# Hybrid trunk in fp32: squares of the keys from the diagonal of the Gram matrix, attention sinks as a 129th score column, another bank for one unit

## The chip, the cores and the metric

The kernel runs on one core of one Trainium2 chip. The metric is the device time of one execution, in microseconds (us). The core's engines are named as in the profile: PE is TensorE (PEld its weight loads), DVE is VectorE, ACT is ScalarE, POOL is GpSimd, and SP is the engine whose queue (SPq) issues nearly all DMAs. The chip may grant TensorE a lower clock; in the profiled run the mean granted clock is 0.999 of full speed.

## What is computed

Two layers of a block with two branches in parallel, then a feed-forward part, for 512 tokens of width 1024, all in float32. Cut to what matters here:

```python
h = rmsnorm(x, pre_mix_g);  proj = h @ w_in          # q k v z, beta, decay | swa q k v | gates A, B
# branch A, gated DeltaNet, 8 heads of 128, per chunk of the sequence:
k = k * rsqrt(sum(k*k) + EPS)                         # l2norm, q likewise
beta = sigmoid(b);  g = cumsum(-exp(a_log) * softplus(a + dt_bias))
L = where(strict, (k*beta) @ k.T * exp(g_i - g_j), 0)
u = triangular_solve(I + L, v * beta);  w = triangular_solve(I + L, k * beta * exp(g))
# branch B, sliding window of 128, 16 query heads on 2 key heads:
m = maximum(max(scores), sink);  p = exp(scores - m)
probs = p / (sum(p) + exp(sink - m));  o = probs @ v
mix = (sigmoid(gate_a) * (o_a @ w_up_dn) + sigmoid(gate_b) * (o_b @ w_up_sw)) @ w_o
x = x + rmsnorm(mix, post_mix_g)
x = x + rmsnorm(relu(rmsnorm(x, pre_mlp_g) @ w_ff1)**2 @ w_ff2, post_mlp_g)
```

## The kernel before

All large products are made in three passes of a shortened fp32 (`mm_a`, L339 to L341): activations and weights are split in a high and a low part, and wh·high, wh·low and wl·high are summed in PSUM, each matmul 128x128 by 512 columns. A unit of 128 output columns has 8 chunks, so 24 such matmuls. The weights come by DMA in tiles of 128x1024 (`wr`); ScalarE makes `wh` from one (L323) and VectorE `wl` (L324), four tiles ahead of use.

A layer runs in stages; times are layer 0's, layer 1's lie 907 us later. Up to 75 us: norm, the projection of branch B's inputs, the decays (`decays`). From 75 to 250 us: the 16 groups of the sliding-window attention (four blocks of 128 tokens, two key heads, two halves of four query heads, numbered 1 to 16 here), mixed by the list MIX with units of the combined projection: K, a head's keys (`k_unit`), G, a unit of gate B (`gb_unit`), A, one of gate A. From 250 to 300 us: the up-projection of branch B (`ps_us`) and two units of gate A. From 300 to 476 us: the eight DeltaNet heads. Then the up-projection of branch A, the output projection and, from 600 us, the feed-forward part.

A group (`att_group`) makes scores for four heads in two banks of the pool PZ, masks them into an SBUF tile M of 128 x 512, takes the row maximum (L904), brings in the sink (`nsk`, its negative; L905, L907, L908, L912), exponentiates with row sums (L910), turns the sums into factors (L913), scales M (L916), has TensorE turn M's four blocks (`ps_pt`, L922), splits the result in `pf_h` and `pf_l`, and multiplies with the values (`ps_o`, L938). The second half of a group, from the transposes on, is written behind the units of the next entry of MIX.

A head's keys: `k_unit` projects (`ps_kp`), convolves, and makes the Gram matrix of the four 128-token blocks (`ps_a`, in the single bank of pool PK). Its diagonal, the keys' squared norms, is taken by four products with the identity with row sums (L740); from it come `irk`, the inverse norm (a pow on GpSimd, L744), and `cj` = beta / (norm² + EPS) (L747, L748). Then `uu` is the Gram matrix times `cj` of the row times the decays D (L752), and is stored (`ud`). When all eight heads are stored, `solve` loads the 32x32 diagonal blocks (`ub`, one DMA of 512 KB in runs of 32 floats) and inverts them column by column on VectorE (pairs L798, L801), between other work, up to the end of the `ps_us` units; the inverses go out to `pd` and come back as `Tc`. For the heads, `d_load` loads `uu` again (`ur`), `d_inverse` completes the inverse by block products on TensorE (`ps_i`), and `d_chain` uses `irk`, `cj` and the decays.

PSUM tiles come from four pools: PM (2 banks, the units), PS (3, general), PK (1), PZ (2). A scheduler orders each engine's instructions by costs of its own out of the program order; where an `Order` object brackets instructions (the four transposes of a group, for one), they stay together. Each engine runs its queue in order, and an instruction that waits holds all behind it; the DMAs of the SP queue are issued in order as well.

Of the kernel before, what the change touches and what calls it, by code (L numbers as in the profile page):

```python
# [15 lines left out]
ALU = mybir.AluOpType  # L16
# [103 lines left out]
def hybrid_trunk(ctx, tc, x, positions, pre_mix_g, dn_conv_w, dn_a_log, dn_dt_bias, dn_norm_g,  # L120
# [139 lines left out]
    gd = dr.tile([32, P], F32, name="gd")  # L260
    sd = dr.tile([H, 512], F32, name="sd")
# [258 lines left out]
    for l in range(depth):  # L520
# [131 lines left out]
        beta = s1("beta", 32)  # L652
# [20 lines left out]
        gc, ngc, neg, egl = (s1(n_, 32) for n_ in ("gc", "ngc", "neg", "egl"))  # L673

        def decays():
# [12 lines left out]
            act(out=egT, in_=gT, func=AF.Exp)  # L688
# [33 lines left out]
        cj, irk = [], []  # L722

        def k_unit(h):
# [55 lines left out]
        def solve():  # L780
# [3 lines left out]
                bass.AP(u0.tensor, u0.offset, [[32 * P + 32, P], [P, 32], [1, 32]]))  # L784
            pb = X4("pb")
# [3 lines left out]
            uv = ub.rearrange("p (j i) -> p j i", j=32)  # L789
            pv = pb.rearrange("p (n i) -> p n i", n=32)  # L790
            for j in range(30, -1, -1):
# [11 lines left out]
                yield  # L803
            dma(pd, pb)
# [65 lines left out]
        def att_group(t, g, e):  # L870
# [12 lines left out]
            M = T[2]("M")  # L883
            for jj in range(2):
# [9 lines left out]
                Mv = c4(M)[:, jj * 2:jj * 2 + 2, :]  # L894
# [9 lines left out]
            nc.vector.tensor_reduce(out=nm, in_=c4(M), axis=AX.X, op=ALU.max, negate=True)  # L904
            tt(out=nm, in0=nm, in1=nsk[:, g, e, :], op=ALU.min)  # L905
            es = sm.tile([P, 4], F32, name="es", bufs=4)
            tt(out=es, in0=nm, in1=nsk[:, g, e, :], op=ALU.subtract)  # L907
            act(out=es, in_=es, func=AF.Exp)  # L908
            for j in range(4):
                act(out=M[:, j * P:(j + 1) * P], in_=M[:, j * P:(j + 1) * P], func=AF.Exp,  # L910
                    bias=nm[:, j:j + 1], accum_out=den[:, j:j + 1])
            tt(out=den, in0=den, in1=es, op=ALU.add)  # L912
            nc.vector.reciprocal(den, den)  # L913
            for j in range(4):
                js = slice(j * P, (j + 1) * P)
                act(out=M[:, js], in_=M[:, js], func=AF.Copy, scale=den[:, j:j + 1])  # L916
# [4 lines left out]
            for j in (3, 0, 1, 2):  # L921
                tr(ps[:, j * P:(j + 1) * P], M[:, j * P:(j + 1) * P], ident)  # L922
# [543 lines left out]
```

## Time and profile before

| | us |
|---|---|
| median of 3 runs | 1830.95 |
| lowest and highest of them | 1829.16, 1831.1 |
| the profiled execution, its own time | 1830.59 |
| its span, first to last instruction | 1828.6 |
| PE busy | 1809.1 (99%) |
| PEld busy | 1503.9 (82%) |
| DVE busy | 1292.1 (71%) |
| ACT busy | 940.9 (51%) |
| POOL busy | 211.2 (12%) |

A matmul is pipelined: the profile draws each longer than the distance to the next, so that PE can be drawn busy where it is not at its peak. The page says that shares are means over stages; the rows further down are of single stages. A wait is put down to the releaser whose event came last. Where a timeline row ends in square brackets, they hold the engine's idle time just ahead of the row and what ended it.

### The profile page before, as it was taken

Reading aid. Unit: us, or ns where it says so; the run is one execution under the profiler, and the core shown is the slowest. Engines: PE = TensorE matmul, PEld = TensorE weight load, DVE = VectorE, ACT = ScalarE, POOL = GpSimd, SP = SyncE. Lnnn points to the kernel's source line nnn. Section 1 sums busy time; section 2 is a strip of 40 time slices with the busy share of each in tenths; the row PEclk is TensorE's granted clock in tenths of the full one; section 3 lists DMA queues with packets and bytes.
Section 4 is the critical chain, followed back from the end, with each engine's and each line's share of the span. In section 5 each row is a group of like instructions: output and inputs, shape, how many; then the busy total and the mean of one; then the engine's idle time right before and its main releaser. Section 6 shows DMA issues by size and latency. Waiting matters only on the chain.

```text
span 1828.6 us, 26748 instructions
## 1 busy us (share of the span) xinstructions
PE 1809.1 (99%) x9598; PEld 1503.9 (82%) x9598; DVE 1292.1 (71%) x2466; ACT 940.9 (51%) x1913; POOL 211.2 (12%) x386
## 2 busy tenths in 40 slices
PE   9999999999999999999999999999999999999998
PEld 8888778888788888888898887888887898888886
DVE  5499796887566758684556997968885568585934
ACT  6678742444434645544347877234444346554442
POOL 0322102221101000000003221022111010000000
PEclk9999999999999999999999999999999999999999
DMA  5633447554453363564245343485545534544631
GB/s 188 202 118 116 115 149 223 179 170 149 124 191 124 96 216 120 168 217 151 93 151 181 104 127 110 167 234 165 160 139 153 172 119 135 174 163 148 233 102 46
DMA packets 146422, 278.48 MB, mean 152 GB/s; under 512 B 33569, under 2 KB 66657, under 8 KB 146290
## 3 DMA queue, kind: packets, MB, share of 16 engines
q1 hardware_dynamic: 145778, 276.75, 47.4%
q8 instruction: 75, 1.23, 0.3%
q14 instruction: 57, 0.47, 0.1%
q0 software_dynamic: 512, 0.03, 0.0%
HBM read 239.38 MB, written 37.36 MB: 151 GB/s over the span
## 4 chain that ended last, share of the span: by engine, by line
PE 84%; DVE 6%; ACT 5%; DMA 3%; issue 1%; POOL 1%; SPq 0%; POOLq 0%; DVEq 0%; ACTq 0%
PE ps_f L340 6%; PE ps_f L339 6%; PE ps_f L341 6%; PE ps_p L402 3%; PE ps_p L404 3%; PE ps_p L400 3%; PE ps_b L388 3%; PE ps_b L387 3%; PE ps_b L389 3%; PE ps_vp L339 2%; PE ps_us L339 2%; PE ps_ud L339 2%; PE ps_vp L341 2%; PE ps_ud L341 2%; PE ps_ud L340 2%; PE ps_us L340 2%
## 5 line engine op out<-in xcount | busy, mean ns | idle before, releaser
L323 ACT CAST wh<-wr 128x1024 fp32r<-128x1024 f32 (+1 forms) x332 | 343.1, 1040 | 542.2 <-PE ps_f L340 145.8
L324 DVE TENSOR_TENSOR wl<-wr,wh 128x1024 fp32r<-128x1024 f32 (+1 forms) x332 | 400.4, 1216 | 303.6 <-ACT wh L323 300.6
L339 PE MATMUL ps_f<-g_h,wh 128*128 128x512 f32 x448 | 174.3, 389 | 0.0
L340 PE MATMUL ps_f<-g_l,wh 128*128 128x512 f32 x448 | 174.3, 389 | 0.0
L341 PE MATMUL ps_f<-g_h,wl 128*128 128x512 f32 x448 | 174.3, 389 | 0.0
L402 PE MATMUL ps_p<-wl,P_h 128*128 128x512 f32 x336 | 131.4, 391 | 0.4 <-DVE wl L324 0.3
L404 PE MATMUL ps_p<-wh,P_l 128*128 128x512 f32 x336 | 130.8, 389 | 0.0
L400 PE MATMUL ps_p<-wh,P_h 128*128 128x512 f32 x336 | 129.5, 389 | 0.0
L437 POOL TENSOR_TENSOR pr<-pq,pw 128x1 f32<-128x1 f32 x16 | 9.8, 613 | 807.6 <-DVE pq L436 807.6
L339 PEld LDWEIGHTS ps_f<-g_h,wh 128*128 128x128 f32 x448 | 84.1, 188 | 17.4
L341 PEld LDWEIGHTS ps_f<-g_h,wl 128*128 128x128 f32 x448 | 84.1, 188 | 17.4
L340 PEld LDWEIGHTS ps_f<-g_l,wh 128*128 128x128 f32 x448 | 84.1, 188 | 17.4
L402 PEld LDWEIGHTS ps_p<-wl,P_h 128*128 128x128 f32 x336 | 63.1, 188 | 15.8 <-DVE wl L324 2.4
L400 PEld LDWEIGHTS ps_p<-wh,P_h 128*128 128x128 f32 x336 | 63.1, 188 | 13.3
L404 PEld LDWEIGHTS ps_p<-wh,P_l 128*128 128x128 f32 x336 | 63.1, 188 | 12.8
L387 PE MATMUL ps_b<-wh,h_h 128*128 128x432 f32 (+1 forms) x192 | 71.1, 370 | 0.0
L388 PE MATMUL ps_b<-wl,h_h 128*128 128x432 f32 (+1 forms) x192 | 70.5, 367 | 0.3 <-DVE wl L324 0.3
L389 PE MATMUL ps_b<-wh,h_l 128*128 128x432 f32 (+1 forms) x192 | 70.2, 366 | 0.0
L293 DVE TENSOR_TENSOR wr<-wr 128x1024 f32<-128x1024 f32 x48 | 58.0, 1220 | 2.6 <-DMA wr<-in_weights_dram 1.9
L340 PE MATMUL ps_qp<-h_l,wh 128*128 128x512 f32 x128 | 54.0, 422 | 0.0
L339 PE MATMUL ps_vp<-h_h,wh 128*128 128x512 f32 x128 | 53.9, 421 | 0.0
L341 PE MATMUL ps_vp<-h_h,wl 128*128 128x512 f32 x128 | 53.6, 419 | 0.0
(359 smaller groups left out, 4873.6 us busy)
## 6 DMA issues: line engine op xcount, KB each, us to landing
wr<-in_weights_dram SPq DMA_DIRECT2D x320, 512.0 KB, 3.5
wr<-in_weights_dram SPq DMA_DIRECT2D x24, 432.0 KB, 3.6
D<-dd SPq DMA_DIRECT2D x32, 256.0 KB, 3.2
xd<-xo SPq DMA_DIRECT2D x12, 512.0 KB, 2.8
xt<-xd SPq DMA_DIRECT2D x24, 256.0 KB, 3.7
D<-gd SPq DMA_DIRECT2D x16, 256.0 KB, 6.5
dd<-D SPq DMA_DIRECT2D x16, 256.0 KB, 3.9
kkd<-kk SPq DMA_DIRECT2D x16, 256.0 KB, 2.0
```

What stands on the lines that cost most here:

```text
L293: tt(out=held[j], in0=held[j], in1=part(i, k, j), op=ALU.add)
L323: nc.scalar.copy(wh[:, :w], wr[:, :w])
L324: sub(out=wl[:, :w], in0=wr[:, :w], in1=wh[:, :w].bitcast(F32), op=ALU.subtract)
L339: mm(ps, lhsT=wh[:, k, :], rhs=hi, start=k == 0, stop=False)
L340: mm(ps, lhsT=wh[:, k, :], rhs=lo, start=False, stop=False)
L341: mm(ps, lhsT=wl[:, k, :], rhs=hi, start=False, stop=k == KT - 1)
L387: mm(pss[t], lhsT=hi[:, tsl], rhs=wh[:, r, :], start=k == 0, stop=False)
L388: mm(pss[t], lhsT=hi[:, tsl], rhs=wl[:, r, :], start=False, stop=False)
L389: mm(pss[t], lhsT=lo[:, tsl], rhs=wh[:, r, :], start=False, stop=k == KT - 1)
L400: mm(pss[t], lhsT=hi[:, c], rhs=wh[:, r, :], start=first, stop=False, skip_group_check=onto)
L402: mm(pss[t], lhsT=hi[:, c], rhs=wl[:, r, :], start=False, stop=False, skip_group_check=onto)
L404: mm(pss[t], lhsT=lo[:, c], rhs=wh[:, r, :], start=False, stop=last, skip_group_check=onto)
```

## The change

The keys' norms are no longer taken per head. `k_unit` makes `uu` = Gram matrix times D in one VectorE product, without `cj`. Since D is 1 on its diagonal, the squared norms stand on the diagonal of `uu`, and `solve` reads them from the blocks `ub` that it loads: it adds EPS (L778 of the new file), stores that through a new DRAM tile `nd`, makes the reciprocal in place (L780), multiplies by beta (`bq`, loaded in the same layout from a new DRAM tile `bd`), scales `ub` by it (L782), and loads `nd` turned as 32x128 (`gT`, a tile used before for the decays). At the end of the column steps TensorE turns that (`ps_nt`), and `irk` and `cj` for all heads are made at once, with one pow on GpSimd of 128x32. `d_load` now has ScalarE scale each block of `ur` by `cj`, four instructions a head. The decays and beta are turned in one transpose of 64 columns (`gcb`), and beta's part is stored to `bd`.

In `att_group` M becomes 128 x 4 x 129. GpSimd copies the sinks into column 128 of the four parts; the maximum and the sums run over 129 columns, and L905, L907, L908 and L912 are gone, as is `nsk`. The scaling and the transposes take the first 128 columns.

The first unit of `ps_us` takes its bank from PS in place of PM.

```diff
         snk = s1("snk", QH)
         dma(snk, sw_sinks[l].partition_broadcast(P))
-        nsk = sm.tile([P, 2, 2, 4], F32, name="nsk", bufs=1)
-        for g in range(2):
-            ts(out=nsk[:, g], in0=snk[:, g * 8:(g + 1) * 8].rearrange("p (j e) -> p e j", e=2),
-               scalar1=-1.0, scalar2=None, op0=ALU.mult)
...
-            tr(ps[:32, :P], gc, ident)
-            gT = sm.tile([32, P], F32, name="gT", bufs=1)
-            nc.vector.tensor_copy(gT, ps[:32, :P])
-            dma(gd, gT)
+            tr(ps[:64, :P], gcb, ident)
+            gT = sm.tile([64, P], F32, name="gT", bufs=1)
+            nc.vector.tensor_copy(gT, ps[:64, :P])
+            dma(gd, gT[0:32])
+            dma(bd, gT[32:64])
...
             u_ = T[5]("uu")
-            sk_ = sm.tile([P, NC], F32, name="ssk")
-            for c in range(NC):
-                sl = slice(c * P, (c + 1) * P)
-                stt(out=u_[:, sl], in0=ps[:, sl], scalar=1.0, in1=ident, op0=ALU.mult,
-                    op1=ALU.mult, accum_out=sk_[:, c:c + 1])
-            ts(out=sk_, in0=sk_, scalar1=EPS, scalar2=None, op0=ALU.add)
-            ir = sm.tile([P, NC], F32, name="irk", bufs=H + 1)
-            ptt(out=ir, in0=sk_, in1=phalf, op=ALU.pow)
-            irk.append(ir)
-            cc = sm.tile([P, NC], F32, name="cj", bufs=H + 1)
-            nc.vector.reciprocal(cc, sk_)
-            tt(out=cc, in0=cc, in1=hc(beta)[:, h, :], op=ALU.mult)
-            cj.append(cc)
-            for c in range(NC):
-                sl = slice(c * P, (c + 1) * P)
-                stt(out=u_[:, sl], in0=ps[:, sl], scalar=cc[:, c:c + 1], in1=d[:, sl],
-                    op0=ALU.mult, op1=ALU.mult)
+            tt(out=u_, in0=ps, in1=d, op=ALU.mult)
             dma(umat(h), c4(u_))
...
+            bq = s1("bq", 32)
+            dma(bq, bd.rearrange("g (b j) -> (g b) j", b=4))
...
+            sq = s1("ssq", 32)
+            ts(out=sq, in0=ub[:, 0:1024:33], scalar1=EPS, scalar2=None, op0=ALU.add)
+            dma(nd.rearrange("g (b j) -> (g b) j", b=4), sq)
+            nc.vector.reciprocal(sq, sq)
+            tt(out=sq, in0=sq, in1=bq, op=ALU.mult)
+            tt(out=uv, in0=uv, in1=sq.unsqueeze(2).broadcast_to([P, 32, 32]), op=ALU.mult)
+            nT = sm.tile([64, P], F32, name="gT", bufs=1)
+            dma(nT[0:32], nd)
...
+            ps = PS("ps_nt")
+            tr(ps[:, 0:32], nT[0:32], ident[:32, :32])
+            nc.vector.tensor_copy(irk, ps[:, 0:32])
+            nc.vector.reciprocal(cj, irk)
+            tt(out=cj, in0=cj, in1=beta, op=ALU.mult)
+            ptt(out=hc(irk), in0=hc(irk), in1=phalf.unsqueeze(1).broadcast_to([P, H, NC]), op=ALU.pow)
...
-            M = T[2]("M")
+            M = T[2]("M", n=4 * (P + 1)).rearrange("p (j w) -> p j w", j=4)
+            nc.gpsimd.tensor_copy(M[:, :, P], snk[:, g * 8 + e:(g + 1) * 8:2])
...
-            nc.vector.tensor_reduce(out=nm, in_=c4(M), axis=AX.X, op=ALU.max, negate=True)
-            tt(out=nm, in0=nm, in1=nsk[:, g, e, :], op=ALU.min)
-            es = sm.tile([P, 4], F32, name="es", bufs=4)
-            tt(out=es, in0=nm, in1=nsk[:, g, e, :], op=ALU.subtract)
-            act(out=es, in_=es, func=AF.Exp)
+            nc.vector.tensor_reduce(out=nm, in_=M, axis=AX.X, op=ALU.max, negate=True)
             for j in range(4):
-                act(out=M[:, j * P:(j + 1) * P], in_=M[:, j * P:(j + 1) * P], func=AF.Exp,
-                    bias=nm[:, j:j + 1], accum_out=den[:, j:j + 1])
-            tt(out=den, in0=den, in1=es, op=ALU.add)
+                act(out=M[:, j], in_=M[:, j], func=AF.Exp, bias=nm[:, j:j + 1], accum_out=den[:, j:j + 1])
             nc.vector.reciprocal(den, den)
...
                     dma(uview(h), umat(h))
+                    for c in range(NC):
+                        act(out=uview(h)[:, c, :], in_=uview(h)[:, c, :], func=AF.Copy,
+                            scale=cj[:, h * NC + c:h * NC + c + 1])
...
-            ps = PM("ps_us")
+            ps = (PM if m else PS)("ps_us")
```

The scheduler makes each engine's order anew. Three places of it follow; a row is a line of the file, the operation, output and inputs, the output's shape and what the row waits for.

ScalarE at group 1, layer 0, before: from the cast of a weight tile to the scaling of M (`kk` is a key convolution).

```order
L323 CAST wh<-wr 128x1024 [waits DMAHW4_49,PE_49,Activation_49]
L908 ACTIVATE es<-es 128x4 [waits DVE_49]
L910 ACTIVATE M,den<-M,nm 128x128 x4
L711 ACTIVATE kk<-ps_kp,cw 128x512 [waits DMAHW7_49,PE_49]
L916 ACTIVATE M<-M,den 128x128 [waits DVE_49,Activation_49]
L916 ACTIVATE M<-M,den 128x128 [waits Activation_49] x3
```

And in the changed file:

```order
L909 ACTIVATE M,den<-M,nm 128x129 [waits DVE_49]
L909 ACTIVATE M,den<-M,nm 128x129 x3
L711 ACTIVATE kk<-ps_kp,cw 128x512 [waits DMAHW0_49,PE_49]
L912 ACTIVATE M<-M,den 128x128 [waits DVE_49]
L912 ACTIVATE M<-M,den 128x128 [waits Activation_49] x3
L325 CAST wh<-wr 128x1024 [waits DMAHW5_49]
```

The cast moved behind the scaling. On TensorE, between the scores of group 2 and the transposes of group 1, there stand 15 matmuls of the next key unit before and 6 now.

VectorE where the solve of layer 0 begins, before (`oT_l` are splits of attention outputs, `qt` the sum of an output's halves):

```order
L904 TENSOR_REDUCE nm<-M 128x4 [waits DVE_49]
L942 TENSOR_TENSOR qt_421<-ps_o,qt_421 64x512 [waits Activation_49]
L905 TENSOR_TENSOR nm<-nm,nsk 128x4 [waits DVE_49]
L412 TENSOR_TENSOR oT_l<-qt_419,oT_h 128x128
L907 TENSOR_TENSOR es<-nm,nsk 128x4 [waits DVE_49]
L412 TENSOR_TENSOR oT_l<-qt_420,oT_h 128x128
L324 TENSOR_TENSOR wl<-wr,wh 128x1024 [waits DMAHW2_49,PE_49,Activation_49]
L798 TENSOR_TENSOR tmp<-ub,pb 128x1 [waits DMAHW4_49,Pool_49]
L801 TENSOR_REDUCE pb<-tmp 128x1 [waits DVE_49]
```

And in the changed file:

```order
L907 TENSOR_REDUCE nm<-M 128x4 [waits DVE_49]
L414 TENSOR_TENSOR oT_l<-qt_418,oT_h 128x128
L414 TENSOR_TENSOR oT_l<-qt_419,oT_h 128x128
L778 TENSOR_SCALAR ssq<-ub 128x32 [waits DMAHW5_49]
L414 TENSOR_TENSOR oT_l<-qt_420,oT_h 128x128 [waits Activation_49]
L910 RECIPROCAL den<-den 128x4 [waits Activation_49]
L780 RECIPROCAL ssq<-ssq 128x32 [waits DMAHW7_49,DVE_49]
L781 TENSOR_TENSOR ssq<-ssq,bq 128x32 [waits DVE_49]
L782 TENSOR_TENSOR ub<-ub,ssq 128x1024 [waits DVE_49]
L326 TENSOR_TENSOR wl<-wr,wh 128x1024 [waits DMAHW0_49,PE_49,Activation_49]
L793 TENSOR_TENSOR tmp<-ub,pb 128x1 [waits DMAHW4_49,DVE_49,Pool_49]
```

The reciprocal of group 13's sums now stands behind the first use of `ub`; behind L793 follow six more solve instructions, a `wl`, the masks of group 14, and `pf_l` of group 13.

TensorE at the first unit of `ps_us`, before (`ps_zp` is the first head's output gate):

```order
L340 MATMUL ps_zp_2940<-h_l_128,wh_2652 128x512
L341 MATMUL ps_zp_2940<-h_h_127,wl_2653 128x512
L339 MATMUL ps_us_2987<-oT_h_2768,wh_2853 128x512 [waits DVE_49,Activation_49]
L340 MATMUL ps_us_2987<-oT_l_2769,wh_2853 128x512
L341 MATMUL ps_us_2987<-oT_h_2768,wl_2854 128x512
```

And in the changed file (`ps_qp` is the first head's queries):

```order
L343 MATMUL ps_qp_2730<-h_h_129,wl_2459 128x512
L341 MATMUL ps_us_2822<-oT_h_2603,wh_2688 128x512 [waits PE_49]
L342 MATMUL ps_us_2822<-oT_l_2604,wh_2688 128x512
L343 MATMUL ps_us_2822<-oT_h_2603,wl_2689 128x512
L341 MATMUL ps_us_2822<-oT_h_2605,wh_2688 128x512
L342 MATMUL ps_us_2822<-oT_l_2606,wh_2688 128x512
L341 MATMUL ps_zp_2775<-h_h_127,wh_2491 128x512 [waits DVE_49,Activation_49]
L342 MATMUL ps_zp_2775<-h_l_128,wh_2491 128x512
```

Five matmuls of the unit now stand ahead of the 24 of `ps_zp`.

## Rows read from the trace of the kernel before

**Rows 1.** Windows, core 0: stretch, length, each engine's busy us (instructions), clock, DMA share.

```profile
75.00:205.00 130.00, 127.63 (x671) 103.84 (x669) 116.10 (x344) 101.28 (x298) 34.49 (x63) 1.00 0.39 118
982.00:1112.00 130.00, 127.26 (x670) 103.75 (x669) 116.12 (x347) 101.62 (x301) 34.15 (x63) 1.00 0.39 118
205.00:250.00 45.00, 44.56 (x208) 35.63 (x208) 34.33 (x84) 31.26 (x89) 5.18 (x7) 1.00 0.30 98
640.00:890.00 250.00, 249.65 (x1100) 205.62 (x1099) 159.64 (x184) 120.91 (x160) 0.00 (x0) 1.00 0.50 167
```

**Rows 2.** Waits of TensorE, whole run: total us, times, longest.

```profile
PE ps_pt L922 <- ACT M L916: 3.9, 6, 0.8
...
PE ps_us L339 <- DVE qq L714: 0.6, 2, 0.3
...
PE ps_a L735 <- DVE uu L752: 0.5, 2, 0.2
...
PE ps_s L892 <- DVE M L900: 0.4, 1, 0.4
```

**Rows 3.** Timeline of TensorE: start, us, line, work, idle before and releaser.

```profile
88.67 0.66 PE L922 MATMUL ps_pt<-ident,M 128*128 128x128 f32 x4 [0.72 <-ACT M L916]
...
107.06 0.66 PE L922 MATMUL ps_pt<-ident,M 128*128 128x128 f32 x4 [0.75 <-ACT M L916]
...
202.05 0.66 PE L922 MATMUL ps_pt<-ident,M 128*128 128x128 f32 x4 [0.51 <-ACT M L916]
```

**Rows 4.** Timeline of VectorE at the first group's chain.

```profile
82.70 0.69 DVE L904 TENSOR_REDUCE nm<-M 128x4 f32<-128x512 f32 x1
83.43 0.16 DVE L905 TENSOR_TENSOR nm<-nm,nsk 128x4 f32<-128x4 f32 x1
...
84.55 1.23 DVE L324 TENSOR_TENSOR wl<-wr,wh 128x1024 fp32r<-128x1024 f32 x1 [0.76 <-ACT wh L323]
...
87.07 0.17 DVE L913 RECIPROCAL den<-den 128x4 f32<-128x4 f32 x1
```

**Rows 5.** Timeline of ScalarE in the same stretch.

```profile
83.47 1.05 ACT L323 CAST wh<-wr 128x1024 fp32r<-128x1024 f32 x1 [1.73 <-PE ps_kp L340]
...
84.53 0.39 ACT L910 ACTIVATE M<-M,nm 128x128 f32<-128x128 f32 x1
...
87.34 1.28 ACT L916 ACTIVATE M<-M,den 128x128 f32<-128x128 f32 x4 [0.46 <-DVE den L913]
```

**Rows 6.** Groups by line: count, busy us, mean ns, idle before.

```profile
L744 POOL TENSOR_TENSOR irk<-ssk,pw 128x4 f32<-128x4 f32 x16 | 18.1, 1129 | 109.7 <-DVE ssk L742 107.3 <-DVE den L913 2.3
L752 DVE SCALAR_TENSOR_TENSOR uu<-ps_a,cj,D 128x128 f32<-128x128 f32 x64 | 17.8, 340 | 0.1
...
L740 DVE SCALAR_TENSOR_TENSOR uu<-ps_a,ident 128x128 f32<-128x128 f32 x64 | 16.1, 282 | 1.7 <-PE ps_a L735 0.8 <-issue 0.8
```

**Rows 7.** Timeline of all engines where layer 1's solve begins (SPq issues DMAs).

```profile
1097.26 0.37 SPq L754 DMA_DIRECT2D ud<-uu  x1
...
1099.62 0.36 SPq L783 DMA_DIRECT2D ub<-ud  x1
...
1105.90 0.15 DVE L798 TENSOR_TENSOR tmp<-ub,pb 128x1 f32<-128x1 f32 x1
```

**Rows 8.** Windows of 1 us behind the issue of ub, columns as before.

```profile
1103.00:1104.00 1.00, 1.00 (x9) 0.93 (x8) 0.97 (x2) 0.78 (x1) 0.00 (x0) 1.00 1.30 128
1104.00:1105.00 1.00, 1.00 (x8) 0.87 (x7) 0.97 (x6) 0.60 (x3) 0.00 (x0) 1.00 0.57 121
```

**Rows 9.** DMA issues: count, KB each, median us from issue to landing.

```profile
ff<-sd SPq DMA_DIRECT2D x16, 2.0 KB, 1.9
```

**Rows 10.** Timeline of all engines ahead of layer 0's block products.

```profile
289.54 3.50 POOL L1050 COPY Pt<-Pc 32x128 f32<-32x128 f32 x8 [0.65 <-DVE Pc L808]
...
295.28 1.06 ACT L323 CAST wh<-wr 128x1024 fp32r<-128x1024 f32 x1 [4.38 <-PE ps_ga L340]
...
300.84 0.21 PE L1018 MATMUL ps_i<-Tc,ur 32*32 32x32 f32 x1
```

More of the change, by code (lines that the diff above doesn't have):

```diff
@@ L260, in hybrid_trunk @@
     gd = dr.tile([32, P], F32, name="gd")
+    bd = dr.tile([32, P], F32, name="bd")
+    nd = dr.tile([32, P], F32, name="nd")
     sd = dr.tile([H, 512], F32, name="sd")
@@ L651, in hybrid_trunk @@
         hc = lambda a: a.rearrange("p (h c) -> p h c", c=NC)
-        beta = s1("beta", 32)
+        gcb = s1("gcb", 64)
+        gc, beta = gcb[:, 0:32], gcb[:, 32:64]
         act(out=hc(beta), in_=ba[:, :, 0:8].rearrange("p t h -> p h t"), func=AF.Exp, scale=-1.0)
@@ L672, in hybrid_trunk @@
         tt(out=hc(lw), in0=hc(lw), in1=nal.unsqueeze(2).broadcast_to([P, H, NC]), op=ALU.mult)
-        gc, ngc, neg, egl = (s1(n_, 32) for n_ in ("gc", "ngc", "neg", "egl"))
+        ngc, neg, egl = (s1(n_, 32) for n_ in ("ngc", "neg", "egl"))
         def decays():
@@ L682, in decays @@
             ps = PS("ps_gt")
-            tr(ps[:32, :P], gc, ident)
-            gT = sm.tile([32, P], F32, name="gT", bufs=1)
-            nc.vector.tensor_copy(gT, ps[:32, :P])
-            dma(gd, gT)
+            tr(ps[:64, :P], gcb, ident)
[3 more added lines that the diff above has]
+            dma(bd, gT[32:64])
             egT = sm.tile([32, P], F32, name="egT", bufs=1)
-            act(out=egT, in_=gT, func=AF.Exp)
+            act(out=egT, in_=gT[0:32], func=AF.Exp)
             dma(egd, egT)
@@ L719, in conv_silu @@
             return a
-        cj, irk = [], []
+        irk, cj = s1("irk", 32), s1("cj", 32)
         def k_unit(h):
@@ L893, in att_group @@
                     mm(o_, lhsT=qh[:, qs], rhs=kTl[:, kw], start=False, stop=True)
-                Mv = c4(M)[:, jj * 2:jj * 2 + 2, :]
+                Mv = M[:, jj * 2:jj * 2 + 2, 0:P]
                 if t == 0:
@@ L903, in att_group @@
             nm = sm.tile([P, 4], F32, name="nm", bufs=4)
[L904 to L908 removed]
+            nc.vector.tensor_reduce(out=nm, in_=M, axis=AX.X, op=ALU.max, negate=True)
             for j in range(4):
[L910 to L912 removed]
+                act(out=M[:, j], in_=M[:, j], func=AF.Exp, bias=nm[:, j:j + 1], accum_out=den[:, j:j + 1])
             nc.vector.reciprocal(den, den)
             for j in range(4):
[L915 to L916 removed]
+                act(out=M[:, j, 0:P], in_=M[:, j, 0:P], func=AF.Copy, scale=den[:, j:j + 1])
             yield
@@ L921, in att_group @@
             for j in (3, 0, 1, 2):
-                tr(ps[:, j * P:(j + 1) * P], M[:, j * P:(j + 1) * P], ident)
+                tr(ps[:, j * P:(j + 1) * P], M[:, j, 0:P], ident)
             together.end()
@@ L1082, in d_turn @@
             kds = sm.tile([P, NC], F32, name="kds")
-            tc.keep_in_program_order(tt(out=kds, in0=cj[h], in1=c4(d)[:, :, P - 1], op=ALU.mult))
+            tc.keep_in_program_order(tt(out=kds, in0=hc(cj)[:, h, :], in1=c4(d)[:, :, P - 1], op=ALU.mult))
             dn["k", h] = k_, by_token(k_, kvx[1][:, h % 2 * 512:(h % 2 + 1) * 512], kxd[h]), kds
@@ L1154, in d_chain @@
                 sl = slice(c * P, (c + 1) * P)
-                stt(out=aT[:, sl], in0=ps[:, sl], scalar=cj[h][:, c:c + 1], in1=d[:, sl],
+                stt(out=aT[:, sl], in0=ps[:, sl], scalar=cj[:, h * NC + c:h * NC + c + 1], in1=d[:, sl],
                     op0=ALU.mult, op1=ALU.mult)
@@ L1160, in d_chain @@
             for c in range(NC):
-                for out_, in_, by in ((vs, vt, irk[h]), (kd, kt, kds)):
+                for out_, in_, by in ((vs, vt, irk[:, h * NC:(h + 1) * NC]), (kd, kt, kds)):
                     act(out=out_[:, c * P:(c + 1) * P].rearrange("p (a i) -> p a i", a=4),
```

## The prediction

> **What bounds the kernel now.** I read the windows first: in the 130 us in which attention, key, gate and up-projection units are mixed, TensorE is busy 127.63 us in layer 0 and 127.26 in layer 1, and in the 45 us behind them 44.56 [rows 1]. So the path is TensorE's own stream, and an engine beside it matters only where a matmul waits for it. The idle time that is to be had there is 2.37 + 2.74 us, and 0.44 in each layer behind it: 5.98 in all. Next the waits: the transposes `ps_pt` stand for the scaled rows M 3.9 us over six waits, the first us unit for `qq` 0.6 over two, `ps_a` for `uu` 0.5 over two, one `ps_s` for M 0.4 [rows 2]. The timeline places three of them in layer 0, at 88.67, 107.06 and 202.05, with 0.72, 0.75 and 0.51 us idle [rows 3].
>
> A wait costs more than the idle shown. A wide matmul is drawn 0.39 us long, but 1,100 of them lie in 250 us, one each 0.227 [rows 1]; so the idle is drawn from a modelled end that lies some 0.17 us behind the place where the next could start. I add 0.17 to each wait: 0.89, 0.92 and 0.68 for the three.
>
> **The sink as a 129th column, and the keys without squares.** Per group the change takes three 128x4 operations off VectorE (such as the 0.16 at 83.43 [rows 4]) and one off ScalarE; per head it takes four products with the identity (282 ns), four scaled ones (340 ns) and a pow on GpSimd (1129 ns) [rows 6], and puts one 128x512 product there, about 0.7 by the reduce over 512 columns at 82.70 [rows 4]. At eight heads that is some 8 × (4 × 0.28 + 4 × 0.34 − 0.7) = 14 us of VectorE per layer before the small ones. None of it is on the path as such: VectorE is busy 116.10 of the 130 us [rows 1]. What counts is the chain from scores to `ps_pt`. Added: a GpSimd copy per group, which fills the column while M's buffer is empty (nothing waits for it at the rate of 63 GpSimd operations in the 130 us [rows 1]), and one column in the reduce and the exps, under 1% of their length.
>
> At the first group the reduce ends at 83.39, but the exps start at 84.53, because the cast `wh` (1.05) got in at 83.47 while two small operations ran; the scaling starts at 87.34, and the transposes at 88.67 [rows 3 to 5]. In the new order the exps follow the reduce and the cast stands behind the scaling: 1.0 us sooner; the reciprocal, at 87.07 behind a `wl` of 1.23 and a reduce, follows the exps, some 0.5 more. But the order also brings them forward: 6 wide matmuls of the key unit stand ahead of them where 15 did, 9 × 0.227 = 2.0 us. Counted from the scores, the chain (mask 0.4 by its width, reduce 0.69, four exps, reciprocal 0.17, one activation over 512 columns that still stands ahead, scaling 1.28) comes to some 5.2 us and the stream ahead (14 wide matmuls, 8 of scores) to 4.1: a wait of about 1.15 where there was 0.89. **This term loses 0.26 per layer.**
>
> At 107.06 the same shortening is about 1.1 us (the small operations stood between products of the keys there, and the reciprocal behind a third one), and the new order takes 1.3 us of other work away; from 6.4 us in both the chain falls to 5.3 and the stream to 5.1. A wait of 0.1 to 0.2 stays of 0.92: **0.82 gained.** At 202.05 I take 0.3 for what stays of 0.68 (below): **0.38.** `ps_a` waits for its bank, whose last reader is now one product and not the fourth of a second four: **0.25 + 0.17 = 0.42.** The first us unit waits for `qq` since both of its pool's banks are held; from another pool it starts ahead of zp: **0.3 + 0.17 = 0.47.** What is late next there is zp, which needs the older of the two banks, free earlier. The `ps_s` wait of layer 1 (0.4 + 0.17 = 0.57) stands behind an M mask on a VectorE queue that is now shorter; I count it as gone.
>
> Against these: two transposes more on TensorE, of 32 columns, each at most the quarter of the 0.66 at 88.67 [rows 3]; I take 0.1 each, 0.2 in all. Sum: 2 × (0.82 + 0.38 + 0.42 + 0.47 − 0.26) + 0.57 − 0.2 = **4.0 us**.
>
> **The solve.** Here waits are added. VectorE now reads the diagonal of `ub` (L778 of the new file) in front of group 13's reciprocal, and turns it in place (L780) only when its store to `nd` has been read; behind these stand the scaling of `ub` (128x1024, 1.23 by the `wl` row [rows 4]), the masks of group 14 and `pf_l` of group 13, which TensorE wants. Before, the first use of `ub` came at 1105.90, 6.3 us behind its issue, and waited for nothing; the DMA share falls from 1.30 to 0.57 at 1104 to 1105, so I take 4.9 for its landing [rows 7, 8]. Counted from the last head's `ps_a`: product and issue 1.1, `ud` landed 2.36 later (1097.26 to 1099.62 [rows 7]), `ub` 4.9 after that, so L778 runs at 8.4 although its turn came near 5.7. The store of 16 KB has no row; the 2 KB `ff` takes 1.9 from issue to landing [rows 9], and I take that. L780 at 10.5, scaled `ub` at 12.0, then two `wl` of 1.23, seven small solve steps of about 0.2, two masks of 0.4 and `pf_l` at 0.7 (by width from the 0.69): 17.3. TensorE's order has 13 transposes at 0.1, 16 score matmuls of half width at 0.12 and 62 wide ones at 0.227 up to the one that reads `pf_l`, also 17.3. So it is a tie, and I put 0.3 there; every microsecond that `ub` or `nd` lands later goes straight into TensorE's time, every one sooner is worth nothing beyond 0.3.
>
> [...]
>
> The end of the solve moves back by some 2.5 us; GpSimd's copies, from 289.54 on (3.50 for each of two blocks), move with it, and the first block product comes at 300.84 [rows 10]: two blocks end near 299, covered. The one pow for all heads, 128x32, lies between 1.13 (the 128x4 form, were all of it fixed) and 8 × 1.13 = 9.0 [rows 6]; I take 5.7, a little over half way up. It stands ahead of these copies. Between the transpose that feeds it and the first block product the order has 72 wide matmuls, 16.3 us; less 2 × 3.5 of copies 9.3 are left, so it costs nothing, at its upper end just so. The scaling of `ur` by `cj`, 4 × 0.32 per head on ScalarE (by 1.28 for four [rows 5]), falls in idle stretches: ScalarE stood 4.38 us idle before the cast at 295.28 [rows 10], 15 of them need 4.8, so that cast slips by under 1 us, with four weight chunks of cover. If the cover went, the price would be those 9 to 10 us per layer. The beta rows ride on a transpose that was there.
>
> **Forecast.** The profiled run took 1830.59; less 4.0 that is 1826.6. It lay 0.36 below the median of 1830.95, so against the median: **1827.0**. A difference of 0.2% (3.7 us) is about what a measurement tells from none here: faster means below 1827.3, slower above 1834.6.
>
> **Rivals.** (a) *The waits only move.* The order is made anew, and it puts the transposes nearer to the scores wherever it believes the chain shorter, as at the first group. If this eats two thirds of the gain, 1829 to 1832. For it: 2.0 us given back there for 1.5 gained. Against it: `ps_a`, us and the third group, which do not depend on it.
>
> (b) *VectorE is held at L778 and L780.* If `ub` lands at 6.3, the bound that the first use gives, and `nd` needs 3.0 with `wr` loads on the queue, `pf_l` is late by 2.5 us per layer. With the chain's gains kept that is 2 × 2.2 more than counted, near 1831.4; with (a) beside it 1835. It decides from about 4 us of added landing, together, on the path of one layer. For it: nothing else is in VectorE's queue that can pass. Against it: `ub`'s own DMA share, falling at 4.9.
>
> (c) *All waits of the stage go.* 5.98 us of idle, plus 0.17 for each of some 16 waits, drawn or too short to be drawn, is 8.7; with all hidden ones up to 10.9: 1820 to 1822. The weight loads speak for it: 103.84 us in the 130 are 79.9%, the dense stretch has 205.62 in 250, or 82.2% [rows 1]; at that density the 130 us would be 126.3 and the 45 us 43.3, in all 10.8 us shorter over both layers. [...] Against it: the stages hold transposes and narrow score matmuls, whose loads differ, and the first group's wait by my count stays.
>
> **How the numbers follow.** Forecast (1824 to 1829) 0.46, (a) 0.24, (b) 0.15, (c) 0.15. Faster by over 0.2%: most of (c) and two thirds of the forecast, 0.44. Slower: (b) where (a) goes with it and GpSimd's pow near its upper end, 0.13. Same: 0.43. The range leaves out half of (c) and two thirds of (b): 1821 to 1833.5.
>
> **What would show it.** In the changed profile: the stage's idle below 4 us in both layers; `ps_pt` waiting once at the first group with 0.9 to 1.0 drawn and hardly at the third; no wait of `ps_a` for `uu`, none of us for `qq`; VectorE some 20 us less busy in the two stages of each layer; L778 idle for about 2.5 us on `ub` and L780 for about 2 on `nd`, and a wait of `ps_o` for `pf_l` of at most half a microsecond; the pow between 3 and 9 us, no idle on TensorE near 303. Wrong if: `ps_o` waits for `pf_l` for over 1.5 us, if the new order brings waits to groups that had none, or if a wait at the head of the next stage (vs, kd) grows by the scaling of `ur`.

## The result, and the profile after

The changed kernel takes 1839.69 us, the kernel before in the same session 1830.12 (medians of six runs each). The ratio is 1.0050, with an interval of 1.0038 to 1.0062: slower by 9.4 to 9.6 us, where some 4 us faster was forecast and 1833.5 was the upper end of the range. The profiled execution shows the same difference, a span of 1838.0 us against 1828.6, so the two traces can be laid side by side.

The windows of the changed kernel, with the columns of [rows 1]: stretch, length, busy us (instructions) of TensorE, its weight loads, VectorE, ScalarE and GpSimd, granted clock, DMA share.

```profile
75.00:205.00 130.00, 126.17 (x661) 101.64 (x660) 103.78 (x196) 101.61 (x293) 29.11 (x66) 1.00 0.39 118
982.00:1112.00 130.00, 126.58 (x664) 102.60 (x663) 102.85 (x189) 100.31 (x286) 31.49 (x73) 1.00 0.38 117
205.00:250.00 45.00, 44.95 (x210) 36.09 (x209) 32.21 (x73) 29.37 (x78) 5.12 (x7) 1.00 0.30 95
255.00:300.00 45.00, 45.00 (x196) 36.36 (x195) 34.03 (x75) 13.66 (x25) 10.60 (x16) 1.00 0.74 224
640.00:890.00 250.00, 249.79 (x1098) 205.67 (x1097) 162.24 (x185) 122.01 (x162) 0.00 (x0) 1.00 0.50 168
```

Against [rows 1], VectorE lost what the change takes away: 116.10 us of 130 became 103.78. TensorE did not get the time: it is busy 126.17 us there where it was busy 127.63, so its idle time rose from 2.37 to 3.83. The 45 us behind did what was hoped, with 44.95 where 44.56 stood. The last two rows hide a second loss. In 255 to 300 us both kernels run the wide matmuls of the us units and of gate A (the changed one also the small transpose `ps_nt`) and TensorE never rests, yet it gets through 196 instructions where the kernel before got through 200. The row of before:

```profile
255.00:300.00 45.00, 45.00 (x200) 37.28 (x199) 32.15 (x66) 8.93 (x9) 8.04 (x22) 1.00 0.75 227
```

The waits of TensorE in the changed kernel, whole run, with the columns of [rows 2]:

```profile
PE ps_pt L918 <- ACT M L912: 3.4, 4, 1.1
...
PE ps_y L1178 <- ACT vs L1161: 2.0, 2, 1.2
PE ps_o L934 <- POOL pc L928: 1.7, 2, 0.9
PE ps_o L934 <- DVE pf_l L414: 1.5, 4, 0.4
PE ps_y L1178 <- DVE rr L1175: 1.1, 2, 0.9
```

The waits of `ps_a`, of the first us unit and of `ps_s` are gone, as forecast. `ps_pt` waits four times, not six. New are four waits for `pf_l`. The waits for the mask `pc` of GpSimd were one of 0.2 us before and are two of 1.7 in all; those of `ps_y`, in the heads, were 1.5 us and are 3.1. The timeline places them in layer 0 (start, length, line, work, idle before and releaser, as in [rows 3]):

```profile
86.61 0.66 PE L918 MATMUL ps_pt<-ident,M 128*128 128x128 f32 x4 [1.13 <-ACT M L912]
...
98.94 0.50 PE L934 MATMUL ps_o<-pf_l,vp 128*128 128x512 f32 x1 [0.40 <-DVE pf_l L414]
...
103.58 0.66 PE L918 MATMUL ps_pt<-ident,M 128*128 128x128 f32 x4 [0.57 <-ACT M L912]
...
128.30 0.50 PE L934 MATMUL ps_o<-pc,vp 128*128 128x512 f32 x1 [0.84 <-POOL pc L928]
...
202.77 0.50 PE L934 MATMUL ps_o<-pf_l,vp 128*128 128x512 f32 x1 [0.39 <-DVE pf_l L414]
```

**Where the 9.4 us lie.** I took the distance from each TensorE instruction's start to the next one's, less what its shape needs in a full stream (0.2267 us for a wide matmul), and split the excess: where the later instruction waits on a semaphore it is a wait, where two wide matmuls follow each other without one it is pace. (A wait counted so is some 0.17 us longer than the idle time that the profile draws; "drawn" below means the latter.) Pace rises from 1.24 to 6.10 us over the us units and the projections behind the heads (+4.9). Waits of the attention stage rise from 6.82 and 6.97 us in the two layers to 8.27 and 8.28 (+2.8). Another +0.7 in both layers together is left over in the attention and us stages, where the two added transposes run. The heads stages show +1.5 (waits of `ps_y` for vs and rr), the start −0.5. The sum is 9.4. The heads' part does not hold still: in the experiment e1 below, whose instruction order is that of the changed kernel, the second heads stage waits 2.93 us, against 4.57 in the changed kernel and 3.16 before.

### The profile page after: what moved, and what is told of

The parts are those of the page before. It is cut to its first block, busy times and chain, and to the rows that moved or that the text cites. A ratio compares the mean times of both kernels' runs of the same rounds, so it can differ in the third digit from the quotient of the medians.

```text
span 1838.0 us, 26490 instructions
## 1 busy us (share of the span) xinstructions
PE 1815.6 (99%) x9600; PEld 1503.8 (82%) x9600; DVE 1268.9 (69%) x2156; ACT 957.5 (52%) x1945; POOL 212.9 (12%) x404
## 4 chain that ended last, share of the span: by engine, by line
PE 86%; DVE 5%; ACT 4%; DMA 2%; issue 1%; POOL 1%; SPq 0%; DVEq 0%; POOLq 0%; ACTq 0%
PE ps_f L341 6%; PE ps_f L342 6%; PE ps_f L343 6%; PE ps_p L404 4%; PE ps_p L406 4%; PE ps_p L402 4%; PE ps_b L389 3%; PE ps_b L390 3%; PE ps_b L391 3%; PE ps_us L341 2%; PE ps_us L343 2%; PE ps_vp L341 2%; PE ps_us L342 2%; PE ps_ud L341 2%; PE ps_ud L343 2%; PE ps_ud L342 2%
## 5 line engine op out<-in xcount | busy, mean ns | idle before, releaser
L909 ACT ACTIVATE M<-M,nm 128x129 f32<-128x129 f32 x128 | 50.0, 393 | 14.0 <-DVE nm L907 13.9
```

## Experiments

**Theory 1: the buffers' places.** The 129th column makes each of `T[2]`'s four buffers 2080 bytes long instead of 2048, and moves `T[3]` and the small tiles behind it. In the kernel before every large tile begins 416 bytes past a multiple of 2048; in the changed one those of `T[2]` and `T[3]` begin at other places. Two rows of either kernel's TensorE timeline inside the us units, with 26 matmuls between the first two and 8 between the last two; nothing waits in either. First the changed kernel, then the kernel before:

```profile
261.66 0.40 PE L342 MATMUL ps_us<-oT_l,wh 128*128 128x512 f32 x1
...
267.91 0.39 PE L342 MATMUL ps_us<-oT_l,wh 128*128 128x512 f32 x1
```

```profile
261.76 0.39 PE L341 MATMUL ps_us<-oT_h,wl 128*128 128x512 f32 x1
...
263.80 0.39 PE L341 MATMUL ps_us<-oT_h,wl 128*128 128x512 f32 x1
```

6.25 us over 27 steps are 0.2315 us each; 2.04 over 9 are 0.2267. The rival: pace has another cause (the changed order, the ur scaling), and places cost nothing.

e1, the changed kernel with buffers of 2112 bytes:

```diff
-            M = T[2]("M", n=4 * (P + 1)).rearrange("p (j w) -> p j w", j=4)
+            M = T[2]("M", n=528)[:, :4 * (P + 1)].rearrange("p (j w) -> p j w", j=4)
```

> The changed kernel with one edit: M's buffer is declared 528 columns wide (2112 B) in place of 516, and the 129-column view is cut from it. Each engine's order is the same as in the changed kernel, row for row; only the addresses of four buffers differ: at 516 columns each takes 2080 B, and two of the four begin at a multiple of 64 B, where every other big tile begins 32 B behind one. Theory A (placement): in the profile of the changed kernel wide matmuls follow each other every 231 ns instead of 227 in the up-projection units, the output projection and parts of the feed-forward, though nothing waits there; the buffers of M are reused there as moving operands. The differences from 227 ns sum to about 4.5 us, so this kernel should take about 1835.2 us. Rival B (waits only): all of the 9.4 us is waits of the new order, and this kernel takes 1839.7.

1836.91 us, ratio 1.0034 [1.0022, 1.0047]: 2.8 us come back, where 4.5 were expected. The pace excess falls from 6.10 to 4.34, so 1.8 of the 2.8 are pace; the rest is of the size of what the second heads stage waits less. Another size is better; it is not free.

e2, the kernel before with buffers of 2080 bytes and nothing else, the same instructions in the same order:

```diff
-            M = T[2]("M")
+            M = T[2]("M", n=516)[:, :512]
```

> The kernel before with one edit: M's buffer is declared 516 columns wide and its first 512 are used, so the four buffers lie at the addresses of the changed kernel. Each engine's order is the same as before, row for row. Theory A (placement): about 4.5 us more than before, 1834.6. Rival B (waits only): as before, 1830.1.

1834.78 us, ratio 1.0025 [1.0016, 1.0035], a loss of 4.4 us with a pace excess of 6.04 against 1.24. Waits of the attention stage stay at 6.82 and 6.89. So the size of a buffer alone, with no computation changed, costs half of the loss.

e8, the kernel before with a pad of 128 bytes ahead of the first M. `T[2]`'s buffers stay 2048 bytes apart and no tile leaves its place within 64 bytes; `T[2]`, `T[3]` and the small tiles just begin 128 bytes later:

```diff
+            if l == 0 and (t, g, e) == (0, 0, 0):
+                nc.gpsimd.memset(up.tile([P, 32], F32, name="pad", tag="pad", bufs=1), 0.0)
             M = T[2]("M")
```

> The kernel before with a pad of 128 B in front of the four buffers of M: these, the four behind them and the small tiles lie 128 B further on; all four stay 2048 B apart and 32 B behind a multiple of 64, and no engine's order changes but for one clear of the pad on GpSimd. If the condition of theory A is the 64 B boundary: as before, 1830.4, wide matmuls every 227 ns. If it is that the moving operands of successive matmuls lie a multiple of 2048 B apart: units that read both groups of buffers slow down, 1832 to 1835.

1834.69 us, ratio 1.0025 [1.0015, 1.0035], a loss of 4.9. The window that ran 200 instructions, first in e8, then in e2:

```profile
255.00:300.00 45.00, 45.00 (x197) 36.77 (x196) 32.32 (x66) 8.91 (x9) 8.21 (x22) 1.00 0.74 225
```

```profile
255.00:300.00 45.00, 45.00 (x197) 36.57 (x196) 32.54 (x66) 8.91 (x9) 8.07 (x22) 1.00 0.74 224
```

The up-projection of branch A is a control within the same runs: its moving operands `yT` lie in `T[4]` to `T[7]`, which none of the edits moves, while `oT` of the us units lies in `T[0]` to `T[3]`. Its stream gets through 156 instructions in 35 us in the kernel before, the changed one, e2 and e8 alike; first the kernel before, then e2:

```profile
495.00:530.00 35.00, 35.00 (x156) 29.00 (x155) 21.90 (x31) 12.00 (x16) 0.00 (x0) 1.00 0.57 183
```

```profile
495.00:530.00 35.00, 35.00 (x156) 28.96 (x156) 21.48 (x30) 11.83 (x15) 0.22 (x1) 1.00 0.57 187
```

For e8's 4.9 us neither a changed spacing of 2048 nor a break of a 64-byte boundary was needed; it was enough that some of the tiles that the matmuls read moved away from the others. In the changed kernel, steps between two wide matmuls last 224 to 241 ns, and nearly the same at the same place of the stream: behind the first us unit of layers 0 and 1, 123 and 137 of 141 steps are within 1 ns of the step 24 matmuls on. What in the addresses sets a step's length stays open: from 255 to 300 us, 36 of the 192 steps between wide matmuls still last 226 or 227 ns.

**Theory 2: the new order of the attention stage makes the waits.** The scheduler orders the stage anew for the changed instructions. The rival: the new instructions themselves make the waits.

e3 does the sinks' column alone, in 2112-byte buffers; e4 the keys' squares alone, without a buffer of another size; e7 the other bank alone:

```diff
-            ps = PM("ps_us")
+            ps = (PM if m else PS)("ps_us")
```

> The kernel before with the sink as a 129th column alone (buffer of M 2112 B, so no tile moves off); keys, solve and the bank as before. Some 5 us of the 9.4 are waits by either theory. If the new order of the groups makes them (rival a of the prediction, waits that move): 1833 to 1835. If the solve's holds make them (rival b): 1828 to 1830, since the shorter chains gain here.

> The kernel before with the keys' part alone (diagonal of the Gram matrix times decays, solve, scaling of ur, one pow, beta with the decays); sinks and the bank as before. If the solve's holds on VectorE make the waits: 1833 to 1835. If the sink's new order makes them: 1829 to 1831.

> The kernel before with the first up-projection unit of branch B in pool PS alone. The prediction's term is 0.47 us per layer (the wait for qq gone), 1829.2 to 1829.4, if that part of the order alone moves. If its being made anew moves other waits too: 1830 to 1833.

e3: 1837.37 us, 1.0038 [1.0024, 1.0051], with 8.16 and 8.58 us of waits in the attention stage and a pace excess of 3.9. In each layer, its transposes of the first and the third group wait 1.4 and 1.3 us (0.9 and 0.9 before), and a matmul of `ps_zp` stands 1.1 us for the cast of its weights, which no term of the prediction had; the wait at the thirteenth group is gone. e4: 1836.63 us, 1.0032 [1.0020, 1.0043], with 10.32 and 10.35 us of waits and no slower pace; its largest are masks of GpSimd. e7: 1828.81 us, 0.9995 [0.9986, 1.0004]: 1.0 us less than before in the medians, about the 0.94 forecast for it, and the wait of the first us unit is gone; but by its interval it can't be told from no change. Both e3 and e4 lie above either range that was set for them. So the large parts each lose alone, the sinks' column in part by its buffers' places.

e5 gives the changed kernel's TensorE the order of the kernel before in the attention stage; e6 gives the kernel before the changed kernel's. Both tie all 772 TensorE instructions of the stage into that order and leave the other engines to the scheduler:

```diff
+        mine = [i for i in traced[k0:] if i.engine == nc.tensor.engine]
...
+        for a, b in zip(perm, perm[1:]):
+            tc.add_manual_dep(mine[b], mine[a].name, mybir.DependencyInfo(
+                mybir.DependencyClass.NoSync, mybir.DependencyReason.DATA), reason="order")
```

> The changed kernel with one addition: the 772 TensorE instructions of the attention stage of each layer are tied into the relative order that the kernel before has there; all else is scheduled anew around them. In the changed kernel, semaphore waits of that stage cost 8.3 us per layer against 6.8 before. Theory C (order): the work of the change would shorten the chains, but the scheduler's order puts the transposes and score products nearer to their inputs, so that the waits remain or grow; with the old order the prediction's gains should appear, 8.3 falling to about 5 per layer: about 6 us faster than the changed kernel, 1833 to 1834 (the buffers' placement still costs its 4 to 5). Rival D (work): the chains are not shorter on the chip (holds on VectorE, GpSimd blocked), and the old order does not help: 1837 to 1840.

> The kernel before with its TensorE instructions of the attention stage tied into the relative order of the changed kernel; no work is changed. Theory C (order): the transposes stand nearer to longer chains, so waits grow by 2 to 4 us per layer: 1834 to 1838. Rival D (work): the order is not what costs, 1830 to 1832.

e5: 1842.43 us, 1.0069 [1.0056, 1.0081]. e6: 1887.77 us, 1.0316 [1.0302, 1.0330]. The two largest waits of TensorE in each, e5 first:

```profile
PE ps_o L935 <- ACT pf_h L414: 5.4, 6, 1.1
PE ps_o L935 <- POOL pc L929: 3.6, 2, 1.8
```

```profile
PE ps_pt L923 <- ACT M L917: 22.7, 14, 2.8
PE ps_s L893 <- DVE qT L867: 8.6, 4, 2.6
```

In e5 no `ps_pt` waits any more: the chain from scores to transposes is really shorter. The wait has gone on to the next step, the split of `ps_pt` and the masks, on engines whose order the scheduler made by itself. e6 shows the other side: with the instructions of the kernel before, the new TensorE order costs 58 us. Both times lie outside either range, so they decide nothing between the two: one engine's order says little without the others'.

e9 therefore gives the changed kernel the old order on TensorE, ScalarE, VectorE and GpSimd together; e10 does that for e4's kernel with e7's bank:

```diff
+        for name, text in RUNS.items():        # tensor, scalar, vector, gpsimd
+            mine = [i for i in traced[k0:] if i.engine == getattr(nc, name).engine]
...
+            for a, b in zip(perm, perm[1:]):
+                tc.add_manual_dep(mine[b], mine[a].name, ...)
```

> The changed kernel, in which TensorE, ScalarE, VectorE and GpSimd all run the attention stage in the order of the kernel before (what both kernels have in common; the new instructions fall in where the scheduler puts them). e5 gave the old order to TensorE alone, and the wait moved to ps_o behind ScalarE and GpSimd, whose orders were still the new ones. Theory (the extra waits of the attention stage are made by the new orders, not by the new instructions): semaphore waits of TensorE in the stage fall from 8.3 us a layer to 6.8 or less, and what is left of the loss is the buffers' places, 4.7 us, less the gains that the parts have (ps_a, ps_us): 1832 to 1835 us. Rival (the new instructions themselves make the waits, whatever the order): the waits stay at 8 us or more a layer and the time at 1837 to 1842.

> The kernel before with the Keys' squares from the diagonal and with the other bank, without the sinks' column, so that no buffer changes its size; the attention stage in the order of the kernel before on the same four engines. e4 (the Keys' squares alone, new order) lost 6 us with waits of 10.3 us a layer in that stage and no slower matmuls. Theory (order): waits of 6.5 us or less a layer, no slower matmuls, the waits of ps_a (0.4 us a layer) and of ps_us (0.5) gone: 1827 to 1829.5 us, a little under the kernel before. Rival (the moved computation itself delays the chain): 1833 to 1837.

e9: 1840.70 us, 1.0058 [1.0044, 1.0071]. e10: 1839.24 us, 1.0051 [1.0039, 1.0064]. Theory 2 as I had put it falls: the waits are 9.4 and 8.9 us in e9, 9.8 and 10.5 in e10, and the times lie in the rival's range (e9) and above it (e10). But nearly all of the difference is one wait in each layer, at the thirteenth group. e9's TensorE, and VectorE ahead of it:

```profile
203.34 0.90 PE L924 MATMUL ps_pt<-ident,M 128*128 128x128 f32 x3 [3.37 <-ACT M L918]
```

```profile
196.13 0.19 DVE L784 TENSOR_SCALAR ssq<-ub 128x32 f32<-128x32 f32 x1
...
198.57 0.35 DVE L786 RECIPROCAL ssq<-ssq 128x32 f32<-128x32 f32 x1 [0.71 <-DMA nd<-ssq]
...
199.18 1.22 DVE L788 TENSOR_TENSOR ub<-ub,ssq 128x1024 f32<-128x1024 f32 x1
...
201.75 0.17 DVE L916 RECIPROCAL den<-den 128x4 f32<-128x4 f32 x1
```

This is where the solve opens. VectorE stands 0.71 us for the transfer of `nd`, turns and scales `ub`, takes the solve's first steps, and only then gets to the reciprocal of `den` that the transposes wait for: an excess of 3.53 and 3.68 us, where the kernel before has 0.67 [rows 3]. Without its thirteenth group e9 waits 5.8 and 5.3 us a layer, the kernel before 6.2 and 6.3, the changed kernel 7.7. So in the old order the shorter chains give back 0.3 and 1.0 us, less than was forecast, and the solve's opening takes 2.9 and 3.0 more than before. The clock that fell behind the wait of layer 0 (last section) cost e9 another 2.0.

e11 and e12 are e9 and e10 with that reciprocal placed ahead of the three new instructions and of the solve's first five steps (told here by tiles; the run gives the order as numbers):

```diff
 # VectorE's order, group 13
-  ssq<-ssq    ssq<-ssq,bq    ub<-ub,ssq    tmp, pb (five steps)    den<-den
+  den<-den    ssq<-ssq    ssq<-ssq,bq    ub<-ub,ssq    tmp, pb (five steps)
```

> e9 with one step of VectorE's order changed: in the thirteenth group the sums' addition-free reciprocal of den goes ahead of the three new instructions that open the Solve (reciprocal of ssq, times bq, and the 1.2 us product on ub) and of its first five steps. In e9 TensorE waited there 3.5 and 3.7 us for the scaling of M, where the kernel before waits 0.67, since den stood behind those and the first of them behind the transfer of nd. Theory: that wait falls to 0.7 us or less in both layers, 5.9 us in all, so 1834 to 1836, and what then still stands over the kernel before is the buffers' places (4.7). Rival: the same instructions now hold back the next unit's scores, the wait moves on by a group, and the time stays at 1838 to 1842.

> The same move in e10 (the Keys' squares and the bank, no sinks' column, no buffer of another size). Waits in the thirteenth group there: 3.55 and 4.39 us against 0.67. Theory: 6.6 us come back and the time is 1831.5 to 1833.5, that is the kernel before within a few tenths of a per cent, since the waits that the change removes (ps_a, ps_us, 1.8 us) and the transposes and scalings that it adds to TensorE's way are about as large as each other. Rival: the wait moves to the next group: 1836 to 1840. If it is under 1829 it beats the kernel before.

e11: 1843.83 us, 1.0077 [1.0065, 1.0090]. e12: 1841.90 us, 1.0060 [1.0047, 1.0074]. Both lie above the rival's range. A moved wait came as the rival had it, though not a group on: the transposes of the thirteenth group are on time (0.76 us of excess in e12), and the wait is now at the next step of the same group, for `pf_l`, which stands behind the solve's opening and steps and the masks and the reduce of the fourteenth. TensorE in e12:

```profile
207.34 0.79 PE L950 MATMUL ps_o<-pf_l,vp 128*128 128x512 f32 x1 [3.07 <-DVE pf_l L420]
```

In these stretches VectorE has no room at all. From 203 to 207 us of e12 it is busy 3.79 of 4.00, with TensorE at 1.27:

```profile
203.00:207.00 4.00, 1.27 (x6) 0.67 (x4) 3.79 (x16) 0.23 (x2) 0.63 (x1) 0.90 0.03 11
```

In this order the opening's work, some 2.5 us with its wait, is paid at that place whichever of the two goes first.

The changed kernel's own order avoids this. Its VectorE rows of the solve's opening:

```profile
193.67 0.18 DVE L778 TENSOR_SCALAR ssq<-ub 128x32 f32<-128x32 f32 x1
...
195.75 0.35 DVE L780 RECIPROCAL ssq<-ssq 128x32 f32<-128x32 f32 x1 [0.50 <-DMA nd<-ssq]
...
196.36 1.22 DVE L782 TENSOR_TENSOR ub<-ub,ssq 128x1024 f32<-128x1024 f32 x1
```

They run 2.5 to 2.8 us earlier than in e9 and the thirteenth group then waits 0.56. Its own extra waits stand at the first, the second and the fifth group (1.30, 0.57 and 1.01 us with the 0.17 added), where e9 has 0.83, 0.39 and 0.1 (and 0.40 at the fourth group). That the scheduler gave those up in exchange for this one is an inference from the places; e3, which has no opening and yet 8.2 and 8.6 us of waits, speaks against it as the only reason. What would settle it, the old order up to the twelfth group with the new one from there on, was not tried, nor was the changed kernel with its large tiles back at their places. Where the waits of the changed kernel stand is read from its trace; whether its order or its instructions make them is not shown.

No version beats the kernel before by more than a measurement can tell. e7 comes nearest.

## Why the prediction was wrong

The forecast's balance was a gain of 4.0 us; what came was a loss of 9.4. Two steps of the sum failed: a term put at nothing, the places of the buffers (4.4 us by e2), and the waits of the attention stage, which were to fall by some 3 and rose by 2.8. Step by step:

- **"One column in the reduce and the exps, under 1% of their length."** This is the step that cost most. The instructions did stay as long, 0.69 us for the reduce over 516 columns and 0.39 for an exp, as in [rows 4, 5]. What the column changed was the size of a buffer, and with it the places of tiles that other stages read, and no term of the sum had those. 4.4 us by e2.
- **The first group, 0.89 to 1.15.** Mechanism right: the cast stands behind the scaling, the exps follow the reduce, and the transposes come at 86.61 instead of 88.67. The wait measured 1.13 drawn, 1.30 with the 0.17 added: the loss is 0.41 for 0.26.
- **The third group, a gain of 0.82.** Mis-sized. 0.57 is still drawn at 103.58, 0.73 with the addition; the gain was 0.2. Which part of the chain or of the stream was counted wrong is open.
- **`ps_a`, 0.42, and us, 0.47.** Both waits went. e7 puts the second at 1.0 us for two layers, against 0.94.
- **`ps_s` in layer 1, 0.57.** Gone, as forecast.
- **The thirteenth group, 0.68 to 0.3.** A tie was forecast between `pf_l` and the stream. `ps_o` waits for `pf_l` there, 0.39 drawn and 0.56 with the addition. L780 stood 0.50 on `nd`, 2.08 us behind L778. But L778 did not stand for `ub`, as it was to do for some 2.5 us: in both layers it ran 6.3 us after the issue of `ub`, with VectorE at work right up to it. The issue in layer 0:

```profile
187.38 0.37 SPq L767 DMA_DIRECT2D ub<-ud  x1
```

  So this run does not show when `ub` landed, the term of 4.9 us stays untested, and that the wait came out near the 0.3 is luck. In other orders the solve's opening costs 3 to 4 us a layer (e9, e12). Rival (b) is nearest to that, and put it at 2.2 us a layer.
- **The pow, 5.7 us on GpSimd, hidden.** It took 5.44:

```profile
289.82 5.44 POOL L804 TENSOR_TENSOR irk<-irk,pw 128x32 f32<-128x32 f32 x1
```

  The copies behind it began at 295.22, and no block product waited. The scaling of `ur` took 389 ns each, for the 320 assumed; no matmul's wait names it. The waits of `ps_y` for `vs` did grow, from 1.1 to 2.0 us, but are 1.2 in e1 with the same order.
- **The copy on GpSimd for which "nothing waits".** Right for the copies of the column (0.26 us each on average), but GpSimd's other work in the stage, the masks, had no term, and it came to hold TensorE. The mask at the fifth group, with VectorE's row under it:

```profile
126.69 1.55 POOL L928 TENSOR_SCALAR_AFFINE_SELECT pc<-pf_l 128x512 fp32r<-128x512 f32 x1 [0.46 <-DVE pf_l L414]
```

```profile
126.54 1.22 DVE L326 TENSOR_TENSOR wl<-wr,wh 128x1024 fp32r<-128x1024 f32 x1
```

  The mask just ahead of it, and the same one in the kernel before at 129.88, take 0.64 us. Here `wl` has begun 0.15 us earlier and the mask ends 0.5 after it. The wait of 0.84 at 128.30 is behind it. In the kernel before 2 of the 48 masks met a `wl` for 0.1 us or more, in the changed one 10, and these took 1.05 us on average. The ends go by what began first: in the six of the ten in which `wl` did, the mask ended 0.5 us after `wl`, whatever its own start; in the other four, `wl` ended 1.08 us after the mask, and took 1.6 to 1.7 us for 1.22. At the fifth group that is 1.55 us for the 0.64 of the mask just ahead; why the two hold each other up, the trace does not show.
- **"If the new order brings waits to groups that had none"** was one of the things that would make the forecast wrong. It did, at the second and the fifth group, and the waits of the attention stage rose by 2.8 us where by the sum they were to fall by some 3. Without the buffers' places the time would by estimate still be near 1835 (1839.7 less 4.4 to 4.9), some 1.5 above the range; so two steps failed, not one. Of this second one the fifth group's wait is traced to the masks; why the others came is open.

Rival (a), that the waits only move, is nearest to this half of the loss, but counted no loss beyond 1832. Rival (c) read the density of the weight loads as room on TensorE. VectorE did become 12 us less busy in the 130 us, and TensorE's weight loads there fell from 103.84 to 101.64: the room was not had by freeing VectorE on average. The waits shown above hang on what VectorE and GpSimd do in one particular microsecond.

## What to carry to other kernels

A change of a tile's size moves every tile that is laid out behind it: lay out the addresses before and after, and if they moved, time the old kernel with the new sizes before anything else (4.4 us here, e2). Work that is taken off a helper engine is worth only what stands ahead of a wait: 12 us less of VectorE in the 130 went with 1.46 us more of idle time on TensorE. Work that is added to it costs its full length where that engine has no slack, as the solve's opening of some 2.5 us did in e9, where its group's wait rose by 2.9 and 3.0. So the place to cost an added instruction is the queue at the microsecond at which it becomes ready, not the busy share of the stage. An order of one engine can't be carried over alone (58 us lost in e6).

## What the runs showed of the hardware

Streams of wide matmuls, with no wait anywhere, ran at 0.2267 us a step in the us units of the kernel before and at 0.224 to 0.241 in the changed one, where some of the tiles that they read lie at other places in SBUF. Moved tiles alone cost 4.4 us (e2) and 4.9 us (e8) of 1830, and neither busy share (45.00 of 45.00 us in the kernel before, e2 and e8) nor wait shows it: the count of instructions in a fixed window does (197 for 200), and the distance of their starts.

A second reading: the wait of 3 us in e12 cost more than itself. TensorE's granted clock was 1.00 in every window of the kernel before that is shown above and in [rows 1]. Behind that wait it fell to 0.50:

```profile
207.00:211.00 4.00, 3.66 (x9) 2.85 (x10) 3.74 (x16) 3.41 (x13) 0.63 (x1) 0.50 0.00 0
```

In the timeline the wide matmuls then follow each other at 0.43 us instead of 0.227:

```profile
209.21 0.63 PE L347 MATMUL ps_ga<-h_h,wh 128*128 128x512 f32 x1
209.63 0.63 PE L348 MATMUL ps_ga<-h_l,wh 128*128 128x512 f32 x1
210.06 0.63 PE L349 MATMUL ps_ga<-h_h,wl 128*128 128x512 f32 x1
```

Ten matmuls ran at that pace, from 208.78 to 213.05 us, and lost 0.2 us each: 2.0 us on top of the wait of 3.07. The changed kernel, whose longest wait in that stage is 1.13 us, stayed at 1.00 there. The length of the idle time alone does not tell whether the clock falls. In e9 it fell to 0.50 behind the wait of 3.37 us in layer 0, and ten matmuls from 204.69 us on lost 2.0 us in all; behind the wait of 3.52 us in layer 1 it stayed at 1.00. The windows of e9 that hold the matmuls behind either wait:

```profile
203.00:207.00 4.00, 3.66 (x11) 3.08 (x12) 3.69 (x13) 2.99 (x13) 1.27 (x2) 0.50 0.00 2
1115.00:1119.00 4.00, 3.33 (x15) 2.24 (x16) 3.76 (x14) 3.45 (x16) 1.27 (x2) 1.00 0.00 0
```
